# An unused 160-byte tile that shifts the later SBUF pools by 160 bytes

## The chip, the cores and the metric

The kernel runs on one core of a Trainium2 chip. The metric is the device time of one execution in microseconds. Before the change three timed runs gave a median of 662.15 us (661.74 to 662.20). One further execution was taken by the hardware profiler; all rows below come from it.

## What is computed

Two layers of a bidirectional encoder over 512 tokens of width 1024, all in float32. Layer 0 mixes tokens by neighbourhood attention, layer 1 by multi-head latent attention (MLA); after each mixer comes a gated per-layer embedding, and at the end one more norm. Cut to its skeleton:

```python
def reference(x, p, norm_g, na_w_in, na_rpb, na_w_out, mla_w_in, mla_q_norm, mla_w_qb,
              mla_kv_norm, mla_w_kvb, mla_w_out, ple_norm, ple_w_gate, ple_w_proj, final_norm):
    for i in range(DEPTH):
        xn = rmsnorm(x, norm_g[i])
        if i % N_MIXERS == 0:
            y = mixer_na(xn, na_w_in[j], na_rpb[j], na_w_out[j])
        else:
            y = mixer_mla(xn, mla_w_in[j], mla_q_norm[j], mla_w_qb[j],
                          mla_kv_norm[j], mla_w_kvb[j], mla_w_out[j])
        h = x + y
        gate = jax.nn.sigmoid(rmsnorm(h, ple_norm[i]) @ ple_w_gate[i])
        x = h + gate * (p[i] @ ple_w_proj[i])
    return rmsnorm(x, final_norm)
```

In both mixers `y` is `(o * silu(z)) @ w_out`, where `o` is the attention's output and `z` a part of the input projection.

## The kernel before

**Number format.** Every float32 operand is split into a high part and a low rest, and a product is the sum of three matmuls: high by high, high by low, low by high. The weights of the two output projections, the two gates and MLA are split into fp32r tiles `whi` and `wlo` of 128 partitions by 1024 columns (`load_w`, L77 to L88: SyncE issues the load of `wraw`, ScalarE writes `whi`, GpSimd writes `wlo`). Layer 0's q, k and v weights and `x` for them are fp16 pairs (`whl`, `xh`, `xl`).

**Stages, in order of time.** The stage `pre` (0 to 46 us) loads x, computes layer 0's embedding projection (pool `pre`, weights and tokens split at L588 and L589) and the first SiLU gates. The heads of layer 0 follow (to about 225 us), then the output projection of layer 0 (`out_proj`, to about 283 us), its gate (`gate_phase`, to about 345 us with the next norm's transposes between), MLA's compression (`mla_c`), its SiLU gates (`z_phase`, 356 to 396 us), the first queries (L696, 396 to 402 us), the sixteen MLA heads (to about 552 us), and the output projection and gate of layer 1.

**Output projection and gate.** These two helpers run the same loop twice each (two layers). For each half `n` of the 1024 output columns four weight tiles are loaded, one for each chunk `c` of 256 input rows, and for each of four token tiles `t` 24 matmuls of 512 columns (`mms`, L221) accumulate into one PSUM bank: for each chunk two by high-high, two by low-high and two by high-low. The stationary operand (128 by 128, loaded into the array by a weight load ahead of each matmul) is the token tile `oT` (tiles `oh`, `ol`, `o1h`, `o1l`) or `hnT`; the moving operand (128 by 512) is the weight half `whi` or `wlo`. The weights come from two places: chunks 0 to 2 of half 0 lie in the pool `wp`, chunk 3 of half 0 and all four chunks of half 1 in the pool `out0` or `out1`, which are opened later:

```python
ws = [self.load_w(a["gate"][layer, n, c], 1024, extra=n == 1 or c == 3) for c in range(4)]
...
hi = pool.tile([P, n if extra else 1024], F32R, name="whi", tag="whi", bufs=self.wxn if extra else 3)
```

So of the 24 matmuls of a token tile in half 0 the six of chunk 3 read their moving operand from the later pool, and in half 1 all 24 do. In layer 1's gate the last token tile of half 1 is done in two column halves (48 matmuls of 256 columns). The order in which the four chunks are taken is the scheduler's.

**What lies where.** SBUF is handed out by pools, one behind the other in the order of their opening; pools that are closed give their room to later ones. A tile takes a multiple of 32 bytes of each partition. `const` begins at byte 16,512 and takes 512 + 32 + 256 bytes, so the next pool begins at 17,312, which is 160 modulo 256. All tiles of `big`, `zp` and `wp` are multiples of 2,048 bytes, so each of them begins at 160 modulo 256. `small` begins at 136,096 (160 modulo 256) and holds 83 places of 32 bytes, 2,656 bytes or 96 modulo 256. The pools opened after it (`pre`, `na`, `out0`, `mla` with `mlac` and `mlah` in it, `out1`) therefore begin at 138,752, which is 0 modulo 256.

| tiles | pool | start modulo 256 before | use |
|---|---|---|---|
| `oh`, `ol`, `o1h`, `o1l`, `hnT`, `x1h`, `x1l`, `xh`, `xl`, MLA's `pt` | `big` | 160 | stationary in the output projections and gates, moving in the z-phases |
| `whi`, `wlo`, `whl`, `wraw` | `wp` | 160 | weights: moving in output projections and gates, stationary in the z-phases and in L696 |
| `whi`, `wlo` with `extra` | `out0`, `out1` | 0 | weights: moving |
| `whi`, `wlo` of the embedding | `pre` | 0 | both operands of layer 0's embedding projection |
| `cT`, `qe`, `qo`, `ke`, `ko` | `mla` | 0 | `cT` moving in L696, stationary in the values; q stationary and k moving in the scores |
| `ex`, `rh`, `rl`, `vt`, `u` | `mlah` | 128 | MLA's heads |
| `whi`, `wlo` with `extra`, `slab_h`, `slab_l`, `c`, `cn` | `mlac` | 128 or 0 | MLA's compression |
| `r`, `gp`, `gn`, `pe`, `sg`, `hg`; `bias`; heads' tiles | `out0`, `out1`, `na` | 0 | residual, gate, bias, heads of layer 0 |
| `xT`, `x` | `pre` | 64, 96 | inputs |

**What sets the order.** Tiles are recorded by a scheduler that simulates the time line; within an engine the instructions then run in the order of the program. All DMAs are issued by SyncE in one order.

Of the kernel before, what the change touches and what calls it, by code (L numbers as in the profile page):

```python
# [14 lines left out]
F32 = mybir.dt.float32  # L15
# [8 lines left out]
P = 128  # L24
# [21 lines left out]
class Trunk:  # L46
    def __init__(self, tc, ctx, a, dbg=None):
        self.tc, self.nc, self.a = tc, tc.nc, a
        self.dbg = dbg or {}
        nc = self.nc  # L50
        ec = ctx.enter_context
        self.const = ec(tc.tile_pool(name="const", bufs=1))
        self.big = ec(tc.tile_pool(name="big", bufs=8))
        self.zp = ec(tc.tile_pool(name="zp", bufs=8))
        self.wp = ec(tc.tile_pool(name="wp", bufs=4))
        self.ps = ec(tc.tile_pool(name="ps", bufs=2, space=PSUM))
        self.ident = self.const.tile([P, P], F32, name="ident")
        self.half = self.const.tile([P, 1], F32, name="half")
        nc.vector.memset(self.half, -0.5)
        self.ones = self.const.tile([P, P], BF16, name="ones")  # L60
        nc.gpsimd.memset(self.ones, 1.0)
        self.hln, self.last_fetch = 0, None
        self.small = ec(tc.tile_pool(name="small", bufs=8))
        self.wx, self.wxn = None, 0
        dram = ec(tc.tile_pool(name="dram", bufs=4, space=bass.MemoryType.DRAM))
        self.spill = [dram.tile([P, D], F32, name=f"spill{t}") for t in range(NT)]
        self.pe = [[dram.tile([P, D], F32, name=f"pe{l}{t}") for t in range(NT)] for l in range(2)]
# [1096 lines left out]
```

## Time and profile before

| | |
|---|---|
| timed runs | 661.74, 662.15, 662.20 us; median 662.15 us |
| the profiled execution's own time | 660.9 us |
| its span, first to last instruction | 659.1 us |
| mean granted TensorE clock | 0.996 |
| VectorE, ScalarE, GpSimd busy | 391.2, 419.6, 328.2 us (59%, 64%, 50%) |
| DMA | 80.18 MB, mean 122 GB/s |

The span is the time between the first and the last instruction of the core; 1.8 us lie around it. In the rows of a time line the columns are the start in us from the span's beginning, the duration in us, the engine, the line of the kernel, the operation, output and inputs by the names of the tiles, the shape, and the number of instructions merged into the row. The modelled duration of a matmul covers its way through the array, and matmuls overlap; the pace is read from the distance of two starts, divided by the number of matmuls between them. An inputs list names the moving and the stationary operand in no fixed order, and a name that both share is given once.

### The profile page before, as it was taken

How to read it: one execution, taken by the hardware profiler on the slowest of the kernel's cores; microseconds unless marked ns; L12 is line 12 of the kernel's file. 1: busy time of each engine (PE TensorE's matmuls, PEld its weight loads, DVE VectorE, ACT ScalarE, POOL GpSimd, SP SyncE). 2: the span in 40 equal slices, each digit the busy share in tenths (PEclk: the TensorE clock that was granted, in tenths of full speed). 3: DMA queues.
4: the chain of work that ended last, by engine and by line, in shares of the span. 5: the costliest groups of instructions: out<-in, count | busy, mean ns of one | idle time of the engine just before them, and what ended most of it. 6: DMA issues, size and time to landing. Idle time of an engine off the chain costs nothing.

```text
span 659.1 us, 10606 instructions
## 1 busy us (share of the span) xinstructions
PE 647.6 (98%) x3720; PEld 499.4 (76%) x3720; DVE 391.2 (59%) x900; ACT 419.6 (64%) x894; POOL 328.2 (50%) x309
## 2 busy tenths in 40 slices
PE   8999999999999999999999999999999999999995
PEld 6876575766756778888899888877777777788884
DVE  6387976867667405644625604888988874234333
ACT  7789977976667723732454635888888886245323
POOL 1341232342327565923054634776959776585311
PEclk9999999999999999999999999999999999999998
DMA  8957132500014055524433345020302122952122
GB/s 286 408 213 282 65 106 84 180 19 1 25 30 153 14 212 220 184 81 140 167 114 105 104 104 160 24 77 25 92 31 66 45 102 95 374 180 91 33 80 95
DMA packets 32756, 80.18 MB, mean 122 GB/s; under 512 B 4416, under 2 KB 9280, under 8 KB 32704
## 3 DMA queue, kind: packets, MB, share of 16 engines
q1 hardware_dynamic: 32704, 79.52, 35.3%
q8 instruction: 29, 0.48, 0.3%
q14 instruction: 23, 0.19, 0.1%
HBM read 67.97 MB, written 8.39 MB: 116 GB/s over the span
## 4 chain that ended last, share of the span: by engine, by line
PE 79%; ACT 8%; DVE 5%; DMA 4%; issue 2%; POOL 1%; SPq 0%; POOLq 0%; DVEq 0%; ACTq 0%
PE ps_mm L221 44%; PE ps_S L221 11%; PE ps_mm L696 6%; PE ps_T L250 5%; PE ps_T L221 3%; PE ps_O L221 2%; PE ps_O L810 2%; ACT whl L158 2%; PE ps_T L543 1%; PE ps_O L447 1%; DMA wraw<-na_z 1%; ACT junk L135 1%; ACT ex L790 1%; DMA x<-x 1%; PE ps_S L507 1%
## 5 line engine op out<-in xcount | busy, mean ns | idle before, releaser
L87 POOL TENSOR_TENSOR wlo<-wraw,whi 128x1024 fp32r<-128x1024 f32 (+5 forms) x81 | 148.2, 1850 | 69.5 <-ACT whi L86 50.7
L86 ACT ACTIVATE whi<-wraw 128x1024 fp32r<-128x1024 f32 (+5 forms) x81 | 65.1, 832 | 48.0 <-PE ps_mm L221 12.5
L792 POOL TENSOR_TENSOR ex<-ex,rc 128x512 f32<-128x512 f32 x64 | 65.9, 1041 | 31.6 <-DVE rc L791 20.9
L221 PEld LDWEIGHTS <-whl 128*128 128x128 f16 x456 | 43.3, 98 | 47.1 <-issue 0.4
L221 PE MATMUL ps_mm<-xh,whl 128*128 128x512 f16 x304 | 73.3, 380 | 0.0
L192 DVE SCALAR_TENSOR_TENSOR pt<-ps_T,pt 128x512 f16<-128x512 f32 (+1 forms) x96 | 62.3, 661 | 14.6 <-ACT pt L191 14.3
L221 PE MATMUL ps_mm<-whi,hnT 128*128 128x512 f32 (+1 forms) x272 | 70.9, 382 | 0.0
L530 POOL TENSOR_TENSOR ex<-ex,rc 128x128 f32<-128x128 f32 (+1 forms) x64 | 34.8, 572 | 49.1 <-DVE rc L526 35.1
L191 ACT ACTIVATE pt<-ps_T 128x512 f16<-128x512 f32 (+1 forms) x96 | 53.4, 574 | 7.3 <-PE ps_T L250 3.8
L221 PEld LDWEIGHTS ps_mm<-whi,hnT 128*128 128x128 f32 x272 | 49.4, 188 | 10.3
L790 ACT ACTIVATE ex<-ps_S,mx 128x512 f32<-128x512 f32 x64 | 43.7, 684 | 9.0 <-DVE mx L788 8.0
L788 DVE TENSOR_REDUCE mx<-ps_S 128x1 f32<-128x512 f32 x64 | 43.6, 687 | 9.6 <-PE ps_S L221 8.2
L221 PE MATMUL ps_mm<-wlo,hnT 128*128 128x512 f32 (+1 forms) x136 | 41.4, 384 | 0.0
L250 PE MATMUL ps_T<-ident,ex 128*128 128x128 f32 x256 | 38.5, 273 | 0.0
L250 PEld LDWEIGHTS ps_T<-ident,ex 128*128 128x128 f32 x256 | 31.3, 140 | 8.2 <-POOL ex L792 1.0
L221 PE MATMUL ps_mm<-xl,whl 128*128 128x512 f16 x152 | 37.1, 379 | 0.0
L97 POOL TENSOR_TENSOR sc<-sc,half 128x1 f32<-128x1 f32 (+2 forms) x11 | 8.2, 744 | 57.1 <-DVE sc L96 57.0
L159 DVE SCALAR_TENSOR_TENSOR whl<-wr,sc,whl 128x512 f16<-128x512 f32 x48 | 34.0, 758 | 2.1 <-ACT whl L158 1.8
L626 DVE TENSOR_TENSOR sg<-pe,sg 128x512 f32<-128x512 f32 (+1 forms) x17 | 12.3, 724 | 37.4 <-ACT sg L625 37.4
L158 ACT ACTIVATE whl<-wr,sc 128x512 f16<-128x512 f32 x48 | 30.9, 712 | 2.3 <-DVE sc L98 2.3
L221 PE MATMUL ps_mm<-whl,xh 128*128 128x256 f16 x224 | 30.7, 273 | 0.8 <-ACT whl L158 0.4
L234 POOL TENSOR_TENSOR rs<-ss,half 128x1 f32<-128x1 f32 x20 | 11.3, 572 | 39.8 <-DVE ss L233 39.8
(368 smaller groups left out, 1556.5 us busy)
## 6 DMA issues: line engine op xcount, KB each, us to landing
wr<-na_qk SPq DMA_DIRECT2D x16, 512.0 KB, 5.6
wraw<-gate SPq DMA_DIRECT2D x16, 512.0 KB, 3.3
pe<-pe SPq DMA_DIRECT2D x24, 256.0 KB, 7.3
wr<-na_v SPq DMA_DIRECT2D x8, 512.0 KB, 7.0
wraw<-na_o SPq DMA_DIRECT2D x8, 512.0 KB, 4.8
wraw<-mla_z SPq DMA_DIRECT2D x8, 512.0 KB, 3.7
wraw<-mla_o SPq DMA_DIRECT2D x8, 512.0 KB, 4.1
wraw<-na_z SPq DMA_DIRECT2D x6, 512.0 KB, 8.3
```

The lines of the kernel that those rows point to most:

```text
L86: nc.scalar.activation(hi[:, c], raw[:, c], AF.Copy)
L87: (rest or nc.gpsimd).tensor_tensor(out=lo[:, c], in0=raw[:, c], in1=hi[:, c].bitcast(F32), op=ALU.subtract)
L158: self.cast = [nc.scalar.activation(h[:, 0, c], r[:, c], AF.Copy, scale=s), nc.vector.scalar_tensor_tensor(h[:, 1, c], r[:, c], s, h[:, 0, ...
L191: self.last_split = nc.scalar.activation(hi, src, AF.Copy, scale=scale)
L192: nc.vector.scalar_tensor_tensor(lo, src, scale, hi, op0=ALU.mult, op1=ALU.subtract)
L221: last = self.last_mm = nc.tensor.matmul(out, l, r, start=i == 0, stop=i == n - 1)
L250: self.last_mm = self.nc.tensor.transpose(t[:, i * P:(i + 1) * P], b, self.ident)
L530: nc.gpsimd.tensor_tensor(out=e, in0=e, in1=rc[:, qt:qt + 1].to_broadcast([P, e.shape[1]]), op=ALU.mult)
L696: self.last_mm = nc.tensor.matmul(PS[key], *terms[i], start=i == 0, stop=i == len(terms) - 1)
L788: nc.vector.reduce_max(mx, sp, axis=AX.X, negate=True)
L790: nc.scalar.activation(ex, sp, AF.Exp, bias=mx, accum_out=sm)
L792: nc.gpsimd.tensor_tensor(out=ex, in0=ex, in1=rc.to_broadcast([P, S]), op=ALU.mult)
```

## The change

One tile is allocated in the pool `small` and never used. It has 40 float32 elements in each partition, 160 bytes.

```diff
         self.small = ec(tc.tile_pool(name="small", bufs=8))
         self.wx, self.wxn = None, 0
+
+        self.small.tile([P, 40], F32, name="gap", tag="gap", bufs=1)
         dram = ec(tc.tile_pool(name="dram", bufs=4, space=bass.MemoryType.DRAM))
```

Nothing is computed with it or written to it. In the built program the tile has no instruction. The rows of all five engines, with the semaphores that they wait for, are word for word those of before, but for the line numbers (two higher behind the new lines). What differs is the start of every tile in the pools opened after `small`: it is 160 bytes higher, 138,912 in place of 138,752 for the first. So those that stood at 0 modulo 256 stand at 160 now, those at 128 at 32, `xT` at 224 and `x` at 0. The tiles of `const`, `big`, `zp`, `wp` and the other small tiles stay where they are.

## Prediction

> **What bounds the kernel now.** I read the page first: the share of each engine, then the chain of work that ended last.
>
> ```profile
> PE 647.6 (98%) x3720; PEld 499.4 (76%) x3720; DVE 391.2 (59%) x900; ACT 419.6 (64%) x894; POOL 328.2 (50%) x309
> ...
> PE 79%; ACT 8%; DVE 5%; DMA 4%; issue 2%; POOL 1%; SPq 0%; POOLq 0%; DVEq 0%; ACTq 0%
> ```
>
> TensorE is busy for 98% of the span and makes 79% of the chain. The change adds and reorders no instruction, so it can act only where an address changes how long something takes. Next come windows by stage (columns: window and length, then busy time and count of PE, PEld, DVE, ACT, POOL, then PEclk, DMA share, GB/s): output projection and gate of layer 0, then the output projection of layer 1; its gate looks the same.
>
> ```profile
> 225.00:283.00 58.00, 58.00 (x291) 45.38 (x290) 23.38 (x29) 27.18 (x40) 43.82 (x24) 1.00 0.51 180
> 283.00:345.00 62.00, 62.00 (x318) 54.17 (x317) 24.92 (x41) 26.49 (x44) 17.03 (x16) 1.00 0.38 125
> ...
> 552.00:606.00 54.00, 54.00 (x265) 42.71 (x264) 17.00 (x29) 24.98 (x35) 35.80 (x19) 1.00 0.59 210
> ```
>
> In each the PE column equals the length of the window, and no other engine comes near it. Here a nanosecond less for each matmul is a nanosecond of the kernel. So the question is whether a matmul's pace depends on where its operands lie. The list of the chain's longest pieces says that it may:
>
> ```profile
> 282.93 32.72 PE ps_mm L221 x141
> ...
> 383.82 12.48 PE ps_mm L221 x55
> ...
> 613.42 32.51 PE ps_mm L221 x140
> ```
>
> These are streams of the same form, fp32r with 512 columns, without a pause. The two gates run at 32.72 / 141 = 232.1 and 232.2 ns each, the z-phase at 12.48 / 55 = 226.9 ns. In the z-phase both operands lie in `big` and `wp`, 160 modulo 256; the gates mix those with weights at 0. The time line of one token tile of layer 0's gate, half 0, separates the two (the last two rows shown belong to the next token tile; the rows left out are of the same two forms):
>
> ```profile
> 290.63 0.62 PE L221 MATMUL ps_mm<-wlo,hnT 128*128 128x512 f32 x2
> ...
> 292.45 1.10 PE L221 MATMUL ps_mm<-whi,hnT 128*128 128x512 f32 x4
> ...
> 293.86 1.09 PE L221 MATMUL ps_mm<-whi,hnT 128*128 128x512 f32 x4
> ...
> 296.17 0.62 PE L221 MATMUL ps_mm<-wlo,hnT 128*128 128x512 f32 x2
> ```
>
> From 290.63 to 292.45 eight matmuls take 1.82 us, 227 ns each: weights in `wp`, so 160 against 160. From 292.45 to 293.86 the six of chunk 3, with weights in `out0`, take 1.41 us, 235 ns each: 0 against 160. Then ten with weights in `wp` again take 2.31 us, 231 ns each, before the pace is back at 227: the slow pace outlasts its cause by some ten matmuls. What other engines do is not the reason:
>
> ```profile
> 292.40:293.80 1.40, 1.40 (x7) 1.13 (x7) 0.00 (x0) 0.00 (x0) 0.00 (x0) 1.00 0.00 0
> 296.00:298.00 2.00, 2.00 (x11) 1.65 (x10) 0.25 (x1) 1.13 (x2) 2.00 (x2) 1.00 0.43 131
> ```
>
> The slow stretch has nothing beside TensorE, no DMA either; the fast one has ScalarE, GpSimd and DMA at work. The clock is 1.00 in both.
>
> **The change part by part.** No instruction, wait or DMA is added or removed, and none is moved past another; the unused tile costs no time. What changes is the pairing of moving and stationary operand.
>
> *Pairs that become 160 with 160.* In half 1 of each output projection and gate all weights are at 0 and the stationary at 160. The steady pace of this pair, and that of two pairs with equal residues, 160 (z-phase) and 0 (embedding of layer 0):
>
> ```profile
> 641.55 1.09 PE L221 MATMUL ps_mm<-whi,hnT 128*128 128x512 f32 x4
> ...
> 644.35 1.09 PE L221 MATMUL ps_mm<-whi,hnT 128*128 128x512 f32 x4
> 387.07 1.98 PE L221 MATMUL ps_mm<-x1l,whi 128*128 128x512 f32 x8
> 394.33 1.98 PE L221 MATMUL ps_mm<-x1h,wlo 128*128 128x512 f32 x8
> 16.17 0.39 PE L221 MATMUL ps_T<-wlo,whi 128*128 128x512 f32 x1
> 19.57 0.40 PE L221 MATMUL ps_O<-wlo,whi 128*128 128x512 f32 x1
> ```
>
> Twelve matmuls from 641.55 to 644.35 take 233.3 ns each, 32 from 387.07 to 394.33 take 226.9, fifteen from 16.17 to 19.57 take 226.7. The last is the row that decides for me: both operands lie there in a late pool at 0 modulo 256, and the pace is the fast one. So 0 is not slow as such; unequal residues are. The count: half 1 has 4 x 24 = 96 such matmuls, chunk 3 of half 0 has 4 x 6 = 24, so 120 in each of four stages, less the 24 that layer 1's gate does in half widths: 456. With 233.3 − 226.7 = 6.6 ns each this is **3.0 us**. The slow pace behind a switch costs 10 x (231 − 227) = 0.04 us, some fourteen times (three or four switches in each stage): **0.6 us**. The 48 half-width matmuls of the last token tile would add 48 x 3.3 ns = 0.16 us if half the columns lose half; no row of equal residues shows this width, so I leave them out.
>
> *The first queries* (L696, `cT` at 0 moving, weights at 160 stationary) are the same case:
>
> ```profile
> 396.14 1.57 PE L696 MATMUL ps_mm<-cT,whi 128*128 128x512 f32 x6
> 401.75 2.02 PE L221 MATMUL ps_mm<-x1h,whi 128*128 128x512 f32 x8
> ```
>
> 24 in 5.61 us are 234 ns each; at 226.7 that saves 0.17 us, and with the slow start of what follows **0.2 us**.
>
> *What stays slow.* A stream of equal residues needs time to become fast after transposes of 128 columns. At 355.90 the z-phase begins behind six of them:
>
> ```profile
> 355.90 2.10 PE L221 MATMUL ps_mm<-x1h,whi 128*128 128x512 f32 x8
> 357.84 1.99 PE L221 MATMUL ps_mm<-x1l,whi 128*128 128x512 f32 x8
> 359.67 0.62 PE L221 MATMUL ps_mm<-x1h,whi 128*128 128x512 f32 x2
> ```
>
> The first eight take 1.94 us, the next eight 1.83, which is still 229 each. The three stages but the last have 24 groups of four transposes between their matmuls; at about 0.02 us each, as the second eight lose against 1.81, this gives back **0.5 us**. What the change brings to the four stages and the queries is then 3.0 + 0.6 + 0.2 − 0.5 = **3.3 us**.
>
> *MLA's heads* are the unknown. Short bursts of scores (0 with 0) and queries (0 with 160) alternate with transposes:
>
> ```profile
> 409.58 0.64 PE L696 MATMUL ps_mm<-cT,whi 128*128 128x512 f32 x2
> ...
> 410.75 0.86 PE L221 MATMUL ps_S<-ke,qe 96*128 96x512 f32 x3
> 411.44 1.09 PE L696 MATMUL ps_mm<-cT,whi 128*128 128x512 f32 x4
> ```
>
> The five queries (with a row of three left out) take 1.17 us, 234 ns each, the three scores 0.69 us, 230 each. After the change all of these are 160 with 160. There are 192 scores (16 heads, four query tiles, three terms) and 132 queries, keys and rope terms, of which some 250 follow another fp32r matmul of that width without a break. If bursts never settle, the gain is 0; if all came down by 6.6 ns, it is 1.65 us. Bursts of three to five are shorter than the ten matmuls that settling took above, so I take 0.1 us, by the row of the scores, which have equal residues today and are not fast.
>
> *Other engines and the DMA.* The splits read and write both kinds of tile. GpSimd's subtraction into `wp` at 200.18 and the three into `out0` and `wp` in a row at 240.93 (7.13 / 3 = 2.38 us) show the same time, and so do loads of 192 KB into `na` at 0 and into `wp` at 160:
>
> ```profile
> 200.18 2.37 POOL L87 TENSOR_TENSOR wlo<-wraw,whi 128x1024 fp32r<-128x1024 f32 x1
> 240.93 7.13 POOL L87 TENSOR_TENSOR wlo<-wraw,whi 128x1024 fp32r<-128x1024 f32 x3
> bias<-na_bias SPq DMA_DIRECT2D x16, 192.0 KB, 2.4
> wraw<-mla_qn SPq DMA_DIRECT2D x8, 192.0 KB, 2.4
> ```
>
> I cost these at nothing. Most loads go to `wp` and do not move at all. What has no cover is the last output and the loads of the first 16 us.
>
> The sum is 3.3 + 0.1 = **3.4 us** of the profiled execution's 660.9 us, to 657.5. The median of the runs stands 1.25 us above that execution; I take the saving from it: 662.15 − 3.4 = **658.8 us**.
>
> [...]
>
> **The rivals.** *The region, not the residue.* All slow pairs also have one operand below byte 138,752 and one above. If that is what counts, the residues change nothing and the time stays at **662.1**. No row of before has a pair in one region with unequal residues, so it is open. Against it stands that the slow pace goes on for ten matmuls with both operands in the low region; that speaks against a plain rule of residues as much.
>
> *Half.* Where the stationary is low and the moving operand high, equal residues may settle only part of the time, as at 231 ns: 1.7 us, **660.4**.
>
> *MLA settles too:* another 1.6 us, **657.2**.
>
> [...]
>
> [...]
>
> **How the numbers follow.** My forecast 0.50; half 0.11; MLA settles too 0.13; the region 0.20; slower 0.06. A measurement of this kernel can tell about 0.2%, 1.3 us, from no change. Faster by more than that: 0.50 + 0.11 + 0.13 = 0.74; within: 0.20; slower: 0.06. The range has to take in the region's 662.1, since without it more than 2 in 10 are left out; below it ends at 657.0, MLA's settling: 657.0 to 662.4. The likeliest case alone is 658.0 to 659.6.
>
> **What would show it.** In the profile after: half 1 of layer 1's gate at 227 ns a matmul in place of 233.3; the two long pieces of the chain near 32.0 us; chunk 3 no slower than its neighbours; the z-phase unchanged at 226.9; the first 45 us unchanged within 0.3 us. I am wrong if half 1 stays at 233 (region), if MLA's scores come below 228 (too small), or if `wraw<-proj` lands later (DMA).

## The result, and the profile after

The changed kernel takes 658.05 us (median of 4 runs, 657.84 to 659.36) against 661.94 us for the kernel before in the same session (4 runs, 661.19 to 662.20). The ratio is 0.9947 with a 95% interval of 0.9930 to 0.9964, so the kernel is faster by about half a per cent. Measured once more beside other kernels (the run `again`), it took 657.62 us against 661.24, ratio 0.9950 [0.9936, 0.9963]. The profiled execution took 658.07 us, with a span of 656.3.

The page of the changed kernel, the lines that answer to the two shown first before: busy time of each engine, then the shares of the chain.

```profile
PE 643.7 (98%) x3720; PEld 499.1 (76%) x3720; DVE 391.6 (60%) x900; ACT 419.8 (64%) x894; POOL 327.8 (50%) x309
...
PE 80%; ACT 8%; DVE 6%; DMA 3%; issue 2%; POOL 1%; SPq 0%; POOLq 0%; DVEq 0%; ACTq 0%
```

TensorE has the same 3,720 matmuls and is busy 3.9 us less (647.6 to 643.7). VectorE, ScalarE and GpSimd move by 0.4 us at most, in both directions. What bounds the kernel has not changed; the same instructions on the bounding engine have become shorter. The same windows as before (window, length, then busy time and count of PE, PEld, DVE, ACT and POOL, then the granted clock, DMA share, GB/s):

```profile
225.00:283.00 58.00, 58.00 (x297) 45.89 (x294) 23.59 (x29) 27.85 (x40) 43.80 (x25) 1.00 0.51 180
283.00:345.00 62.00, 62.00 (x324) 55.01 (x324) 24.99 (x41) 26.35 (x44) 17.84 (x16) 1.00 0.40 128
...
552.00:606.00 54.00, 54.00 (x266) 43.17 (x264) 18.08 (x30) 24.71 (x34) 37.16 (x19) 1.00 0.60 214
```

TensorE still fills each window without a gap, at the same clock, but more matmuls fit into the first two: 297 for 291, and 324 for 318. The chain's long pieces say it more exactly, since they hold the same instructions before and after (start, duration, engine, output, line, count):

```profile
282.76 32.01 PE ps_mm L223 x141
...
382.94 12.49 PE ps_mm L223 x55
...
611.28 31.77 PE ps_mm L223 x140
```

The two gate pieces have lost 0.71 and 0.74 us (from 32.72 and 32.51) and now run at 227.0 and 226.9 ns a matmul. The z-phase, whose operands did not move, takes 12.49 us for 12.48. TensorE's time line of the changed kernel shows where inside the gates the time was; first layer 0, half 0, then layer 1, half 1 with its last matmuls in half widths (start, duration, engine, line, operation, tiles, shape, count):

```profile
288.09 1.07 PE L223 MATMUL ps_mm<-whi,hnT 128*128 128x512 f32 x4
...
298.97 1.07 PE L223 MATMUL ps_mm<-whi,hnT 128*128 128x512 f32 x4
...
636.08 1.07 PE L223 MATMUL ps_mm<-whi,hnT 128*128 128x512 f32 x4
...
641.52 1.07 PE L223 MATMUL ps_mm<-whi,hnT 128*128 128x512 f32 x4
...
642.88 0.64 PE L223 MATMUL ps_mm<-whi,hnT 128*128 128x256 f32 x4
643.35 0.40 PE L223 MATMUL ps_mm<-wlo,hnT 128*128 128x256 f32 x2
643.59 0.64 PE L223 MATMUL ps_mm<-whi,hnT 128*128 128x256 f32 x4
```

The 48 matmuls from 288.09 to 298.97 take 10.88 us, 226.7 ns each. They hold two groups of chunk 3, which took 235 ns before, and the 231 ns behind them is gone as well. In half 1 the 24 matmuls from 636.08 to 641.52 take 226.7 ns each, where they took 233.3. Six half-width ones take 0.71 us. The rows of before have 0.72 for the same six, and over all 48 the mean distance of two starts is 119.9 ns in both traces:

```profile
645.75 0.64 PE L221 MATMUL ps_mm<-whi,hnT 128*128 128x256 f32 x4
646.23 0.40 PE L221 MATMUL ps_mm<-wlo,hnT 128*128 128x256 f32 x2
646.47 0.64 PE L221 MATMUL ps_mm<-whi,hnT 128*128 128x256 f32 x4
```

To say what each stage gained, the same instruction is looked up in both time lines: the transposes behind the start, the group of values of layer 0's heads just ahead of the output projection (one more group follows 12 us later), the two ends of the first queries, and the first of the last 24 values of MLA's heads. Before (the ends of the first queries stand in the prediction):

```profile
28.23 0.60 PE L250 MATMUL ps_T<-ident,ssq 128*128 128x128 f32 x4
...
223.23 1.34 PE L447 MATMUL ps_O<-pt,vt 128*64 128x256 f16 x24
...
555.44 0.40 PE L810 MATMUL ps_O<-pt,vt 128*64 128x512 f16 x1
```

After:

```profile
28.73 0.60 PE L252 MATMUL ps_T<-ident,ssq 128*128 128x128 f32 x4
...
223.79 1.34 PE L449 MATMUL ps_O<-pt,vt 128*64 128x256 f16 x24
...
395.27 1.52 PE L698 MATMUL ps_mm<-cT,whi 128*128 128x512 f32 x6
...
400.71 1.98 PE L223 MATMUL ps_mm<-x1h,whi 128*128 128x512 f32 x8
...
554.09 0.40 PE L812 MATMUL ps_O<-pt,vt 128*64 128x512 f16 x1
```

| up to | before, us | after, us | later (+) or earlier (−) | gained in this stretch |
|---|---|---|---|---|
| transposes behind the start | 28.23 | 28.73 | +0.50 | −0.50 |
| values of layer 0's heads, ahead of its output projection | 223.23 | 223.79 | +0.56 | −0.06 |
| gate piece, layer 0 (output projection done) | 282.93 | 282.76 | −0.17 | 0.73 |
| first queries (gate and z-phase done) | 396.14 | 395.27 | −0.87 | 0.70 |
| behind the first queries | 401.75 | 400.71 | −1.04 | 0.17 |
| first of the last values of MLA's heads | 555.44 | 554.09 | −1.35 | 0.31 |
| gate piece, layer 1 | 613.42 | 611.28 | −2.14 | 0.79 |
| end of the span | 659.1 | 656.3 | −2.8 | 0.7 |

From the start of layer 0's output projection on the gain is 0.73 + 0.70 + 0.17 + 0.31 + 0.79 + 0.7 = 3.4 us. This one execution lost 0.5 us in its first 28 us, before any of the pairs concerned runs. The runs below ask whether that belongs to the change.

### The profile page after: what moved, and what is told of

Same layout as the page of the kernel before. It is cut to its first block, busy times and chain, and to the rows that moved or that the text cites. A ratio compares the mean times of both kernels' runs of the same rounds, so it can differ in the third digit from the quotient of the medians.

```text
span 656.3 us, 10606 instructions
## 1 busy us (share of the span) xinstructions
PE 643.7 (98%) x3720; PEld 499.1 (76%) x3720; DVE 391.6 (60%) x900; ACT 419.8 (64%) x894; POOL 327.8 (50%) x309
## 4 chain that ended last, share of the span: by engine, by line
PE 80%; ACT 8%; DVE 6%; DMA 3%; issue 2%; POOL 1%; SPq 0%; POOLq 0%; DVEq 0%; ACTq 0%
PE ps_mm L223 44%; PE ps_S L223 12%; PE ps_mm L698 6%; PE ps_T L252 6%; PE ps_T L223 3%; PE ps_O L812 3%; PE ps_O L223 2%; ACT whl L160 2%; PE ps_T L545 1%; PE ps_O L449 1%; DMA wraw<-na_z 1%; ACT junk L137 1%; PE ps_S L509 1%; DMA xT<-xT 1%; DVE xT L966 1%
## 5 line engine op out<-in xcount | busy, mean ns | idle before, releaser
L527 ACT ACTIVATE ex<-ex,nm 128x128 f32<-128x128 f32 (+1 forms) x64 | 30.2, 475 | 1.0
```

## The experiments

Two theories were held against each other. A: a fp32r matmul of 512 columns goes at 227 ns if its moving and its stationary operand start at equal residues modulo 256, and at about 233 if not. B: what counts is where the moving operand itself starts, whatever the stationary one does. The prediction's region rival (one operand below the small tiles, one above) stands beside them, and the question which stages carry the gain. No run adds or reorders an instruction; each only allocates tiles that nothing uses, or allocates one in another place. Each engine has the same instructions in the same order in all fourteen traces. "Late" means opened after the pool `small`. The kernels before, in the three sessions, had medians of 661.29, 661.38 and 661.24 us.

### Only the output projections and gates move

```diff
             with tc.tile_pool(name=f"out{layer}", bufs=4, reuse_waits="tile") as pool:
+                pool.tile([P, 40], F32, name="gap", tag="gap", bufs=1)
                 self.wx, self.wxn = pool, 5
```

The tile in `small` is absent, so `pre`, `na` and `mla` stay at 0.

> The 160-byte tile stands at the head of the pools out0 and out1 alone; pre, na and MLA's pools stay at 0 as before. Theory A: the four stages of projection and gate gain 3.0 us, the first queries and MLA nothing; half 1 of the gates runs at 227 ns, the queries stay at 234. Ratio 0.9955 (0.5% less than before would be the whole change). If the half microsecond that the changed kernel lost in its first 28 us is a price of the moved loads of pre, it isn't paid here and the first 28 us are those of before.

Measured: 658.5 us, ratio 0.9955 [0.9942, 0.9967]. The chain of this run:

```profile
282.81 32.02 PE ps_mm L221 x141
...
382.86 12.48 PE ps_mm L221 x55
...
611.67 31.78 PE ps_mm L221 x140
```

The gate pieces are those of the changed kernel, and so is nearly the whole gain. The first queries go from 395.18 to 400.79 us, 5.61 us or 234 ns each, as slow as before, and the first of the last values of MLA's heads starts at 554.53, which makes 153.7 us from there, also as before. The transposes behind the start begin at 28.72 us, as late as in the changed kernel, though `pre` has not moved.

### All but the output projections and gates move

The reverse: the changed kernel, and 96 bytes more at the head of `out0` and `out1`, which brings these back to 0 modulo 256.

```diff
+        self.small.tile([P, 40], F32, name="gap", tag="gap", bufs=1)
...
             with tc.tile_pool(name=f"out{layer}", bufs=4, reuse_waits="tile") as pool:
+                pool.tile([P, 24], F32, name="gapo", tag="gapo", bufs=1)
```

> The changed kernel with out0 and out1 moved back to 0 modulo 256: only the first queries and MLA's heads keep the change. Theory A: the projections and gates are as before (half 1 at 233 ns), the first queries fast, MLA's heads 0.3 us faster; together 0.5 us less than before, or nothing where the start costs 0.5: ratio 0.999 to 1.000.

Measured: 660.97 us (10 runs), ratio 0.9995 [0.9986, 1.0004], not to be told from no change. Its chain:

```profile
282.65 32.72 PE ps_mm L223 x141
...
612.86 32.51 PE ps_mm L223 x140
```

To the hundredth these are the pieces of before. The weights of these pools stand 256 bytes further up than before here, and on the same side of `small` as in the changed kernel. From that one they differ by 96 bytes, and the pace is slow. The first queries (396.01 to 401.45 us, 227 ns each) and MLA's heads (from there to 554.83, 153.4 us) are as fast here as in the changed kernel; that half microsecond is too little to show in the total.

### The first stage back at 0

The changed kernel with 96 bytes at the head of `pre`, so that everything loaded in the first 16 us starts where it did modulo 256, and only the later pools stay moved.

```diff
         with tc.tile_pool(name="pre", bufs=4, reuse_waits="tile") as pool:
+            pool.tile([P, 24], F32, name="gapp", tag="gapp", bufs=1)
```

> The changed kernel with the pool pre moved back to 0 modulo 256 (96 bytes at its head). Both operands of the embedding projection are at 0 then, equal residues as with 160, so theory A expects the same gain as the changed kernel in all later stages. If the half microsecond lost in the first 28 us of the changed kernel's profile is the price of loads that land at 160, this kernel is 0.5 us faster than the changed one, ratio 0.994; if it was chance, the ratio is that of the changed kernel, 0.9947, and the first 28 us vary by half a microsecond from run to run.

Measured: 658.37 us, ratio 0.9953 [0.9940, 0.9965], which includes the changed kernel's ratio. In its time line the transposes behind the start stand no earlier than in the changed kernel:

```profile
28.87 0.60 PE L252 MATMUL ps_T<-ident,ssq 128*128 128x128 f32 x4
```

Over the profiled executions of all these kernels the same row begins at 28.23 (before), 28.72 (`outonly`), 28.87 (`pre0`), 29.13 and 29.98 with `pre` at 0 modulo 256 (the last two are `wp256` and `allzero`, below), and at 28.15 (`notout`), 28.73 (changed), 28.78 (`again`), 29.02 and 29.74 with `pre` at 160 (`all160` and `wp0`, below). With `pre` at 32, 64, 96 and 128 (below) it begins at 28.52, 28.38, 28.88 and 28.62. The sets for 0 and 160 cover the same range. So the +0.5 us of the table is what single executions differ by, and no price of the moved loads shows.

### Weights in `wp` moved, the stationary ones not

Here 96 bytes at the head of `wp` bring its tiles from 160 to 0, and 64 bytes in `small` bring the late pools to 160, as in the changed kernel. The tokens in `big` stay at 160. This makes half 1 an equal pair and makes two pairs unequal that never were: half 0's chunks 0 to 2, and the z-phases, where both operands lie in the low region.

```diff
+        self.wp.tile([P, 24], F32, name="gapw", tag="gapw", bufs=1)
...
+        self.small.tile([P, 16], F32, name="gap", tag="gap", bufs=1)
```

> The pool wp alone is moved to 0 modulo 256 (a 96-byte unused tile at its head, and 64 bytes in place of 160 in small, so that the later pools stay at 160 as in the changed kernel). Theory A, unequal residues of moving and stationary operand are slow: in the z-phases (moving 160, stationary now 0, both in the low region) the pace goes from 227 to about 233 ns, 229 matmuls, 1.5 us; in half 0 of the projections and gates chunks 0 to 2 (moving now 0, stationary 160) go to 233, 288 matmuls, 1.9 us; the first queries go back to 233, 0.2 us. Together about 3.7 us above the changed kernel, near 661.8 us, ratio to before 0.999 to 1.001. Theory B, only the moving operand's own start counts (0 slow, 160 fast): the z-phases stay at 227 and the time is about 2 us above the changed kernel, 660 us, ratio 0.997.

Measured: 661.95 us (10 runs), ratio 1.0008 [0.9998, 1.0017]: the whole gain is gone again. The time line, first in the z-phase of MLA, then in half 1 of layer 1's gate:

```profile
386.96 2.03 PE L224 MATMUL ps_mm<-x1h,whi 128*128 128x512 f32 x8
...
392.58 2.03 PE L224 MATMUL ps_mm<-x1h,whi 128*128 128x512 f32 x8
...
636.47 1.07 PE L224 MATMUL ps_mm<-whi,hnT 128*128 128x512 f32 x4
...
641.91 0.39 PE L224 MATMUL ps_mm<-whi,hnT 128*128 128x512 f32 x1
```

In the z-phase 24 matmuls take 5.62 us, 234 ns each, where they took 227 in every kernel that left `wp` alone. The moving operand, `x1h` and `x1l`, starts at 160 as before; only the stationary weights have moved. That ends theory B. Both operands lie below `small`; that ends the region. In half 1 of the same kernel 24 matmuls take 5.44 us, 226.7 ns each. The slow pairs were exchanged for others, and the time came out where it was, as theory A had it (661.8 us).

### Everything at 0

The changed kernel with 96 bytes more in `const`, so that `big`, `zp`, `wp`, `small` and all late pools but those inside `mla` start at 0.

```diff
         self.half = self.const.tile([P, 1], F32, name="half")
+        self.const.tile([P, 24], F32, name="gapc")
...
+        self.small.tile([P, 40], F32, name="gap", tag="gap", bufs=1)
```

> 96 unused bytes in const beside the 160 in small: big, zp, wp and all later pools stand at 0 modulo 256. Theory A, equal residues: all fp32r streams run at 227 ns as in the changed kernel, ratio 0.993 to 0.996. Theory B, a moving operand at 0 is slow: every stream including the z-phases runs at 233 ns, which is 229 x 6.6 ns = 1.5 us and more above the kernel before, ratio 1.002 or more.

Measured: 658.62 us, ratio 0.9956 [0.9942, 0.9971], that of the changed kernel. Its time line in the same two places:

```profile
386.80 1.98 PE L224 MATMUL ps_mm<-x1l,whi 128*128 128x512 f32 x8
...
394.05 1.98 PE L224 MATMUL ps_mm<-x1h,wlo 128*128 128x512 f32 x8
...
636.73 1.07 PE L224 MATMUL ps_mm<-whi,hnT 128*128 128x512 f32 x4
...
639.45 0.84 PE L224 MATMUL ps_mm<-whi,hnT 128*128 128x512 f32 x3
```

32 in 7.25 us and 12 in 2.72: 226.6 and 226.7 ns. So 160 is not better than 0; equal (226.6 to 226.9 ns) is better than unequal (233 to 235).

### Which differences are slow

The same change with smaller tiles in `small`. The late pools then start at 32, 64, 96 or 128 modulo 256 against tokens at 160.

```diff
-        self.small.tile([P, 40], F32, name="gap", tag="gap", bufs=1)
+        self.small.tile([P, 8], F32, name="gap", tag="gap", bufs=1)
```

(16, 24 and 32 elements in the other three.)

> 64 bytes in place of 160: the later pools stand at 64, the weights in wp and the tiles in big at 160, a difference of 96 bytes modulo 256 like before's, with the other sign. Theory A with a period of 256 expects half 1 of the gates at about 233 ns as in before. Were the period 32, every difference would be equal and this kernel as fast as the changed one, 227 ns.

> 96 bytes: a difference of 64 modulo 256. If the period of what must be equal is 64, half 1 of the gates runs at 227 ns; if it is 128 or 256, at 231 to 235.

> 128 bytes: a difference of 32 modulo 256. Periods of 64, 128 and 256 all expect 231 to 235 ns in half 1 of the gates; a period of 32 expects 227.

> 32 bytes in place of 160: a difference of 128 modulo 256 between the weights of out0 and out1 and the stationary tiles. If the period is 128, half 1 of the gates runs at 227 ns; if it is 256, at 231 to 235 as with differences of 32, 64 and 96.

To these belongs a run that moves `wp` and all that follows by a full 256 bytes against `big`:

```diff
+        self.wp.tile([P, 64], F32, name="gapw", tag="gapw", bufs=1)
```

> The kernel before with 256 unused bytes at the head of wp: big stays, wp and all later pools move up by 256 bytes, all residues modulo 256 are those of before, and big against wp differs by 256 modulo 512. If the period is 256, the z-phases (big against wp) stay at 227 ns; if it is 512, they go to 233 ns, which costs 1.5 us.

Each was profiled once. The long pieces of the chain, of the smallest tile first, then of the largest, then of the 256-byte move:

```profile
282.68 32.57 PE ps_mm L223 x141
```

```profile
283.22 32.64 PE ps_mm L223 x141
```

```profile
283.27 32.72 PE ps_mm L222 x141
...
384.16 12.48 PE ps_mm L222 x55
```

| late pools modulo 256 | distance to 160 | gate piece of layer 0, us | ns a matmul (141) | half 1 of layer 1's gate, ns a matmul | one run's time, us |
|---|---|---|---|---|---|
| 0 (before) | 160, or 96 the other way | 32.72 | 232.1 | 233.3 | 660.9 |
| 32 | 128 | 32.57 | 231.0 | 233.3 | 660.17 |
| 64 | 96 | 32.75 | 232.3 | 234.2 | 661.16 |
| 96 | 64 | 32.64 | 231.5 | 233.3 | 661.05 |
| 128 | 32 | 32.64 | 231.5 | 233.3 | 660.61 |
| 160 (changed) | 0 | 32.01 | 227.0 | 226.7 | 658.07 |

The gate piece mixes half 0 and half 1. The expectations speak of half 1 alone, and its last 24 matmuls of full width show it. With the late pools at 64 they take 5.62 us, from the first of these rows to the second; at 32, 96 and 128 they take 5.60:

```profile
638.98 1.09 PE L223 MATMUL ps_mm<-whi,hnT 128*128 128x512 f32 x4
...
644.60 1.10 PE L223 MATMUL ps_mm<-whi,hnT 128*128 128x512 f32 x4
```

Every distance tried that is not 0 is slow, at nearly the same price (231.0 to 232.3 ns in the gate piece, 227.0 at 0); nothing grows or falls with it. In the 256-byte move the z-phase mixes `big` and a `wp` that stands 256 bytes further from it, and keeps its 12.48 us. So a full 256 counts as equal, while 32, 64, 96 and 128 do not.

The matmuls of half the width do not follow this order. With the late pools at 96 six of them take 0.68 us, less than the 0.71 and 0.72 at equal residues:

```profile
647.28 0.62 PE L223 MATMUL ps_mm<-whi,hnT 128*128 128x256 f32 x4
...
647.96 0.62 PE L223 MATMUL ps_mm<-whi,hnT 128*128 128x256 f32 x4
```

Over the 48 of them the mean is 113.6 ns there, 118.2 to 118.8 with the late pools at 32, 64 and 128, and 119.9 in the kernel before and in the changed one. Why this is so was not asked.

### MLA's bursts

In the changed kernel the queries at the start of MLA's heads became faster and the scores did not, though both have equal residues now:

```profile
408.45 0.62 PE L698 MATMUL ps_mm<-cT,whi 128*128 128x512 f32 x2
408.91 0.84 PE L698 MATMUL ps_mm<-cT,wlo 128*128 128x512 f32 x3
409.59 0.86 PE L223 MATMUL ps_S<-ke,qe 96*128 96x512 f32 x3
410.28 1.07 PE L698 MATMUL ps_mm<-cT,whi 128*128 128x512 f32 x4
```

Five queries take 1.14 us, 228 ns each (234 before); three scores take 0.69, 230 each, as before. Later in the heads transposes stand between such bursts, and their operands stood at other residues, `ident` at 128 and MLA's head tiles at 32; this might have been what kept the rest slow. The last variant puts both at 160; beside it the changed kernel ran once more (`again`, whose times stand in the result).

```diff
-        self.ident = self.const.tile([P, P], F32, name="ident")
...
+        self.ident = self.const.tile([P, P], F32, name="ident")
...
+                pool.tile([P, 32], F32, name="gapm", tag="gapm", bufs=1)
                 with tc.tile_pool(name="mlac", bufs=2, reuse_waits="tile") as cpool:
```

> The changed kernel with two more moves: ident is allocated last in const (160 in place of 128), and 128 unused bytes stand ahead of mlac and mlah, so that MLA's ex, rh, rl, vt, u and the extra weights of mla_c go from 32 to 160. Then all tiles that TensorE reads start at 160. If the slow bursts of MLA's heads (232 ns in the changed kernel) come from the transposes with unequal residues between them, the heads' 250 unbroken pairs go to 227 ns and the kernel is 1.3 us faster than the changed one, ratio to it 0.998. If they come from the interruption itself, nothing changes.

> The changed kernel once more, beside the next kernel on the same chip: ratio 0.993 to 0.997 to before, span's first 28 us anywhere from 28.2 to 30.1.

Measured: 658.5 us, ratio 0.9957 [0.9945, 0.9970], beside the 0.9950 of the changed kernel run with it. The same place in its time line:

```profile
409.01 0.62 PE L698 MATMUL ps_mm<-cT,whi 128*128 128x512 f32 x2
409.47 0.84 PE L698 MATMUL ps_mm<-cT,wlo 128*128 128x512 f32 x3
410.15 0.86 PE L223 MATMUL ps_S<-ke,qe 96*128 96x512 f32 x3
410.85 1.07 PE L698 MATMUL ps_mm<-cT,whi 128*128 128x512 f32 x4
```

1.14 us for the five and 0.70 for the three: here nothing moved. Over the whole stage a little did. Two scores of 96 rows in a row start 230.5 ns apart on average, 233.9 in the changed kernel, and the stretch from the end of the first queries to the first of the last values takes 153.27 us for 153.38. That is 0.1 of the 1.3 us, so the residues of the transposes are not what mainly keeps the scores slow.

Two other explanations can be held against the trace of the changed kernel. No transpose runs there between 406.15 and 412.82 us, and the scores in that stretch still take 230 to 233 ns each; so they are slow without an interruption by transposes as well. Nor is it the 96 rows of these scores, for every second head has scores of 128 rows:

```profile
454.22 0.95 PE L223 MATMUL ps_S<-ko,qo 128*128 128x512 f32 x3
455.00 1.31 PE L698 MATMUL ps_mm<-cT,whi 128*128 128x512 f32 x5
...
458.56 0.95 PE L223 MATMUL ps_S<-ke,qe 96*128 96x512 f32 x3
459.35 1.09 PE L698 MATMUL ps_mm<-cT,whi 128*128 128x512 f32 x4
```

Right behind transposes three scores of 128 rows take 0.78 us and three of 96 rows 0.79. What keeps the scores slow stays open.

No variant is faster than the changed kernel by more than the intervals; `pre0`, `outonly`, `allzero` and `all160` all lie within them.

## Why the prediction was right

A time of 658.8 us was predicted and 658.05 measured. The saving was put at 3.4 us; it is 3.9 by the medians of the first session, 3.6 by those of `again`, and 3.4 in the profiled execution behind its slow start.

**Unequal residues, not the value 0.** This was the step on which all hung, and it rested on one row, the embedding at 0 with 0. It holds in both directions: unequal pairs inside the low region become slow (234 ns in the z-phase of `wp0`), pairs across `small` become fast once they are equal (226.7 ns in half 1 of the changed kernel), and all at 0 is as fast as all at 160 (658.62 us in `allzero`, 658.5 in `all160`).

**The terms.** The four stages of output projection and gate were to bring 3.0 + 0.6 − 0.5 = 3.1 us, and the table has 0.73 + 0.70 + 0.79 + 0.7 = 2.9. The first queries were put at 0.2 and gave 0.17. The 48 half-width matmuls were left out, and rightly, 0.72 us for six before and 0.71 after. The 10-matmul settling behind chunk 3 went with its cause. Of the three terms behind 3.1 only the sum was measured, so a fault in one may hide one in another. That the whole comes to 3.4 us in the profile as well is in part luck: here 0.2 us too little, in MLA's heads 0.2 too much.

**MLA's heads** were the term that was mis-sized: 0.1 us predicted, 0.31 measured. The prediction argued from the scores, which were equal already and stayed at 230, that bursts shorter than ten matmuls would not settle. The queries with `cT` gained all the same: from 234 to 228 ns in the burst of five shown above. Over the whole stage the gain is smaller: where one matmul with `cT` is followed at once by another wide one, their starts are 231.9 ns apart on average, 234.5 before (101 such distances in each trace). So a part of the gain comes in short bursts already. The size repeats: from the end of the first queries to the first of the last values MLA takes 153.37 to 153.40 us in five traces with equal pairs (the changed kernel, `again`, `notout`, `pre0`, `allzero`) and 153.69 to 153.73 in the kernel before, `outonly`, `wp0` and `wp256`. One trace does not fit: with the late pools at 128 the pairs are unequal and it takes 153.35, which no run explains. The full 1.6 us of the rival that MLA settles too was not reached, and its sign, scores below 228 ns, did not come.

**The first 45 us** were to stay within 0.3 us, and 28 us into the profiled execution 0.5 had been lost. One sign that was to speak for a slower kernel came with it: the first load `wraw<-proj` of the chain, which took 4.09 us before, takes 4.28 in the changed kernel. But it takes 4.52 in `outonly` and 4.55 in `wp256`, where `pre` stands at 0, and 3.74 in `wp0`, where it stands at 160. The mark was too narrow: that start lies between 28.15 and 29.98 us in fourteen profiled executions of kernels that have the same work there, with no order by the residue of the pool.

**The rivals.** The region fell with `wp0` and `notout`. "Half" fell with 226.7 ns in half 1. A slower kernel, by loads that cost more where they now begin, had been given 0.06. No run shows such a cost: with `pre` back at 0 nothing changed that can be measured (0.9953 [0.9940, 0.9965] beside 0.9947 and 0.9950 with `pre` at 160). With the same instructions in the same order, the starts of TensorE's two operands in SBUF decide between 227 ns a matmul (z-phase of the changed kernel) and 234 (z-phase of `wp0`).

**What stays open** is why a matmul takes longer when its two operands start at different places modulo 256; no run shows it. Nor do equal residues settle everything: the scores stay at 230 ns or more with them, and the half-width matmuls are fastest at a distance of 64 (113.6 ns, against 119.9 at 0).

## What to carry to other kernels

Where a kernel is bound by long streams of fp32r matmuls of 512 columns, look at where the moving and the stationary operand start in SBUF modulo 256 bytes, and try equal starts: an unused tile ahead of a pool does it without an instruction of its own, and brought half 1 of layer 1's gate from 233.3 to 226.7 ns a matmul here, 2.8%. Check every pair that shares an operand, since moving one pool can trade one slow stage for another, as `wp0` did (ratio 1.0008). A pace that is read from a time line as a distance of starts over a count shows such a thing at once, where a mean over a stage hides it (232.1 ns over the gate piece, in which groups at 227, 231 and 235 lie).

## What was not expected of the hardware

That the price is nearly the same for every unequal distance tried, 32, 64, 96 and 128 bytes: between 231.0 and 232.3 ns in the gate piece, against 227.0 at distance 0, and 233.3 or 234.2 in half 1, against 226.7. That the width matters so much: fp32r matmuls of 256 columns take 119.9 ns at distance 160 and at 0, and 113.6 at a distance of 64. And that a slow pair slows the equal ones behind it: 231 ns for some ten matmuls behind chunk 3 before, and 226.7 in the same place once chunk 3 is equal.
